# A two-layer hybrid encoder on one core: in the first half of the feed-forward, raw low halves of the weights go to GpSimd, unions of product banks precede the next weights' sums, and ScalarE copies the second bank whole

## The chip, the core and the metric

The kernel runs on one core of one Trainium2 chip, in one launch. The time is the device time of one execution in microseconds (us). The core's engines work beside each other, each through its own list of instructions in order: TensorE (PE; PEld is its loading of weights), VectorE (DVE), ScalarE (ACT), GpSimd (POOL) and SyncE (SP), which issues the DMA transfers. They wait for each other through semaphores. SBUF is the on-chip memory; PSUM is the memory into which TensorE writes its products, in banks of 128x512 fp32 numbers. GpSimd's instructions here have all their operands in SBUF; VectorE and ScalarE read and write both memories.

## What is computed

The input is x of shape (1, 512, 1024) in fp32, and the parameters of two layers. The feed-forward part, in which the change lies, closes each layer:

```python
        hf = rms_norm(x, ffn_norm_g[l])
        u = depthwise_conv(hf @ ffn_w_up[l], ffn_conv_w[l], ffn_conv_b[l])
        u_gate, u_val = u[..., :D_FF], u[..., D_FF:]
        x = x + (jax.nn.silu(u_gate) * u_val) @ ffn_w_down[l]
```

D_FF is 2816, so the up projection is 1024 to 5632 and the down projection 2816 to 1024. Ahead of it stand, in each layer, an RMS norm, a combined input projection, three branches (multi-head latent attention, grouped-query attention, centred mean pooling), their gated merge and an output projection.

## The kernel before

**Layout.** The stream x is held transposed in SBUF as XM, eight tiles of 128 channels by 512 tokens. The normed input of the up projection is held as HH (high half) and HL (low half).

**Products in three parts.** Each fp32 operand is split in two fp32r numbers, high and low, and a product is taken as high by high, high by low and low by high. The weights come from HBM as raw pieces (128x512, two to a transfer of 512 KB; three transfers' room, filled by SP). ScalarE copies a raw piece into `wh` (L272), and VectorE or GpSimd makes `wl` as raw minus `wh` (L280). L272 and L280 are helpers through which nearly every copy and every two-operand operation goes, so groups are told apart by their tiles.

**Seven products for eight.** Most of the feed-forward's pieces are used in a Strassen-like form (`w_seven`): a piece holds a 2x2 block of 128x128 tiles and is used with seven products, not eight. Its first three blocks are used as they are: ScalarE copies them (`wh<-raw`, 128x384), and `rest` makes their low halves (`wl<-raw,wh`, 128x384), on the engine that `pick(W_BIAS)` chooses. The other four weights are sums of blocks: `first` has ScalarE copy one block into a PSUM bank (`ps_mi` or `ps_S`, in turn), `both`, `third` and `fourth` build the sums there on VectorE (one 128x256 and two 128x128 operations), `hi` copies the bank to `wh` (128x512, ScalarE) and `lo` makes `wl<-ps_mi,wh` or `wl<-ps_S,wh` (128x512, VectorE). In the names of the order, `wh180_0` and `wl180_0` are the raw part of piece 180, `wh180_1` and `wl180_1` its sums.

**Halves.** The 22 blocks of D_FF are done in two halves, 10 and 12 (HALVES). In each half the up projection runs first, then the down projection over four pairs of output tiles (m = 0, 2, 4, 6): five pieces for each m in the first half, six in the second. `products` (matmuls at L1911) runs 21 matmuls of 128x256 for each piece into four PSUM banks b0 to b3, which are drawn from a ring of six (two each of acc, ST and AV). With the first piece of an m the banks are taken in the order b0, b1, b2, b3, b2 at its 13th matmul and b3 at its 19th. The last piece of m = 0 runs the products in the order 2, 1, 3, 6, 5, 4, 7 (`late`), with the activations that come last used last.

**Unite.** When an m is done, `unite` adds its four banks into two XM tiles and gives the banks back to the ring: XM += b0 (b0 free); ScalarE copies the first half of b1 into u; u2 (the second half of u) = first half + second half of b1 on VectorE (b1 free); XM += b2 in two operations (b2 free); b3 += u2; XM += u on GpSimd; XM += b3 (b3 free). For the last m of the program an `early` form has all of it on VectorE.

**Back loads.** In the first half the normed input is fetched again during the down projection (`again(m)`): four tiles `back` for each m, split into HH and HL or tf by ScalarE and GpSimd, spaced by GAP.

**Activations.** `up_evac` takes the up projection's output through convolution and gate and splits it into `ah` tiles; `turns` makes two of the splits (of t34 and t12), for the last block of D_FF on VectorE, else on GpSimd.

**What sets the order.** A planner runs at build time. It keeps a clock for each engine with estimated costs, takes steps of `chain`s from a heap as their inputs are expected to be ready, and emits instructions in that order; data dependencies then become semaphore waits. On the chip each engine follows the emitted order.

Of the kernel before, what the change touches and what calls it, by code (L numbers as in the profile page):

```python
# [63 lines left out]
GAP = 2.0  # L64
# [93 lines left out]
class Clock:  # L158
# [5 lines left out]
    def __init__(self):  # L164
        self.now, self.n, self.heap, self.busy = 0.0, 0, [], False
        self.fin, self.free, self.ready = 0.0, {}, {}
        self.source = self.last = None
        self.gives_way = {}
        self.locked = (0.0, 0.0)
# [50 lines left out]
    def chain(self, *steps, after=0.2):  # L220

        def go(n, source=None, since=None):
# [4 lines left out]
            if late and max(late) > self.now:  # L227
                self.at(max(late) - self.now, lambda: go(n))
                return
# [84 lines left out]
def trunk(ctx: ExitStack, tc: tile.TileContext, x, w, prm, gb, cst, pad, out):  # L314
# [99 lines left out]
    def w_seven():  # L414
# [20 lines left out]
        def rest():  # L435
            e = pick(W_BIAS)
            e.tensor_tensor(los[0][:, :384], r[:, :384], f(his[0][:, :384]), ALU.subtract)
            done("wa", j)
            if j + 1 == len(pieces) or pieces[j + 1][0] > sl:
                at(max(0.0, ck.free[e.kind] - ck.now) + D_FREE, lambda: w_upto(sl + 1 + RAW))  # L440
# [17 lines left out]

        chain(([("sums", j * L // len(pieces))] + ([("w", j - 2)] if seven[j - 2] else []), first), rest, after=0.0)
# [202 lines left out]
    def layer(l, sq, xsrc):  # L662
# [206 lines left out]
        def set_keys():  # L869
            for _, kb in KAB:  # L870
                G.memset(f(kb[64:P, :T]), 0.0)
                G.memset(f(kb[64:65 if "gqa" in PLAN else 96, :T]), 1.0)

        at(0.5, set_keys)
# [918 lines left out]
        def up_evac(c, part, acc, tag, scaled):  # L1793
# [77 lines left out]
            def turns():  # L1871
# [3 lines left out]
                      *split(new[4][:, :T], new[5][:, :T], t34[:, :T], eng=eng), end(2), after=0.0)  # L1875
# [12 lines left out]
        def products(right_, banks_, first, late=False):  # L1888
            j = st["use"]
            his, los = (lambda z: (z[:2], z[2:]))(wnext())  # L1890
# [81 lines left out]
        def unite(m, banks_, then, early=False):  # L1972
# [11 lines left out]
            chain(lambda: A.activation(p1, b1[:, :256], AF.Copy), after=0.0)  # L1984
            if early:
                chain(add(x0, x0, b0), add(u2, p1, b1[:, hi_]), add(x0[:, hi_], x0[:, hi_], b2[:, hi_]), add(x0, x0, u[:, :T]),
# [3 lines left out]
            chain(add(x0, x0, b0), lambda: free(t0), add(u2, p1, b1[:, hi_]), lambda: free(t1),  # L1990
                  add(x0[:, hi_], x0[:, hi_], b2[:, hi_]), add(x1, x1, b2), lambda: free(t2),
                  add(b3[:, :256], u2, b3[:, :256]),
# [29 lines left out]
        for c0, c1 in HALVES:  # L2022
            room[:] = spare
            for n_, (c, part) in enumerate(_ups(c0, c1)):
# [15 lines left out]
            for m in range(0, KC, 2):  # L2040
# [4 lines left out]
                for k in range(c0, c1 - 2 * PLAIN * end_, 2):  # L2045
                    products(right_of(k // 2), banks_, k == c0, m == 0 and k == c1 - 2)
# [211 lines left out]
```

## Time and profile before

| | |
|---|---|
| median of 3 runs (lowest to highest) | 1538.01 us (1537.58 to 1538.58) |
| the profiled execution's own time | 1538.08 us |
| its span, first to last instruction | 1536.3 us |
| DVE, ACT, POOL busy | 1206.2, 974.5, 1120.1 us (79%, 63%, 73%) |
| mean granted TensorE clock | 0.999 |
| HBM traffic over the span | 118 GB/s |
| chain that ended last, by engine | PE 75%, DVE 12%, ACT 6%, POOL 3%, issue 3%, DMA 1% |

The profiled execution lies 0.07 us from the median, and 1.78 us of its time lie outside the span. In the rows of the timeline, the first number is the start in us from the span's start, the second the duration (of a row with x2 or more, from the start of the first to the end of the last), then engine, line, operation, tiles written <- tiles read, shape, and how many. What stands in square brackets is idle time of the engine before the row, and what ended it. A matmul's duration overlaps with the next one's: the time that it costs is the distance from start to start.

### The profile page before, as it was taken

What the parts mean: (1) busy time and instruction counts of PE and PEld (TensorE: products, weight loads), DVE (VectorE), ACT (ScalarE), POOL (GpSimd) and SP (SyncE); (2) the same over time, 40 slices, a digit from 0 to 9 for tenths busy, and PEclk for the clock granted to TensorE, in tenths of its full rate; (3) what the DMA queues carried; (4) which work ended last, traced back from release to release, by engine and by line L of the source; (5) the groups of instructions that cost most, each with busy time, mean ns of one, the idle gap of its engine ahead of it and who ended that gap; (6) DMA issues with size and microseconds to landing.
All of it is one profiled execution on the core that took longest, in us unless ns stands there. A gap on an engine that the chain in (4) does not pass through costs nothing.

```text
span 1536.3 us, 25158 instructions
## 1 busy us (share of the span) xinstructions
PE 1519.1 (99%) x8390; PEld 1325.6 (86%) x8390; DVE 1206.2 (79%) x2386; ACT 974.5 (63%) x1961; POOL 1120.1 (73%) x1077
## 2 busy tenths in 40 slices
PE   9999999999999999999999999999999999999999
PEld 8888788788889899999998877888888899989998
DVE  6778889986578896778857788899865788867786
ACT  6557776664567665666654587766636677656763
POOL 4865986854689787675779659868547897967753
PEclk9999999999999999999999999999999999999999
DMA  6432234424344453333444322344243444533332
GB/s 219 117 111 78 76 92 139 130 91 132 105 140 147 148 176 106 94 103 109 133 129 136 102 70 76 112 134 130 79 151 96 141 148 138 182 107 100 95 121 84
DMA packets 91954, 183.56 MB, mean 119 GB/s; under 512 B 21936, under 2 KB 43696, under 8 KB 91824
## 3 DMA queue, kind: packets, MB, share of 16 engines
q1 hardware_dynamic: 91680, 181.94, 38.0%
q8 instruction: 66, 1.08, 0.3%
q14 instruction: 64, 0.52, 0.1%
q10 hardware_dynamic: 144, 0.01, 0.0%
HBM read 159.89 MB, written 22.02 MB: 118 GB/s over the span
## 4 chain that ended last, share of the span: by engine, by line
PE 75%; DVE 12%; ACT 6%; POOL 3%; issue 3%; DMA 1%; SPq 0%; ACTq 0%; DVEq 0%; POOLq 0%
PE ps_acc L491 24%; PE ps_AV L491 16%; PE ps_ST L1911 8%; PE ps_ST L491 8%; PE ps_acc L1911 7%; PE ps_AV L1911 6%; PE ps_S L491 2%; PE ps_mi L491 2%; ACT wh L272 2%; DVE nmt L290 1%; DVE wl L280 1%; DVE vt L284 1%; DVE XM L280 1%; DVE pl L280 1%; POOL qa L280 1%
## 5 line engine op out<-in xcount | busy, mean ns | idle before, releaser
L280 POOL TENSOR_TENSOR wl<-raw,wh 128x512 fp32r<-128x512 f32 (+3 forms) x487 | 579.7, 1200 | 306.3 <-ACT wh L272 267.0
L272 ACT ACTIVATE wh<-raw 128x512 fp32r<-128x512 f32 (+2 forms) x521 | 290.9, 577 | 21.1 <-PE ps_ST L491 11.3
L491 PE MATMUL ps_acc<-HH,wh 128*128 128x512 f32 x504 | 196.9, 391 | 0.1
L491 PE MATMUL ps_acc<-HL,wh 128*128 128x512 f32 x504 | 196.5, 390 | 0.0
L491 PE MATMUL ps_acc<-HH,wl 128*128 128x512 f32 x504 | 196.3, 389 | 0.0
L491 PEld LDWEIGHTS ps_acc<-HH,wl 128*128 128x128 f32 x504 | 94.6, 188 | 19.9
L491 PEld LDWEIGHTS ps_acc<-HH,wh 128*128 128x128 f32 x504 | 94.7, 188 | 19.7 <-DVE gt L280 0.6
L491 PEld LDWEIGHTS ps_acc<-HL,wh 128*128 128x128 f32 x504 | 94.7, 188 | 18.9
L491 PE MATMUL ps_AV<-HH,wh 128*128 128x512 f32 x248 | 96.7, 390 | 0.0
L491 PE MATMUL ps_AV<-HL,wh 128*128 128x512 f32 x248 | 96.6, 390 | 0.0
L491 PE MATMUL ps_AV<-HH,wl 128*128 128x512 f32 x248 | 96.5, 389 | 0.0
L272 ACT ACTIVATE wh<-ps_S 128x512 fp32r<-128x512 f32 x79 | 47.3, 598 | 49.2 <-DVE ps_S L280 37.8
L272 ACT ACTIVATE wh<-ps_mi 128x512 fp32r<-128x512 f32 x79 | 47.3, 598 | 46.5 <-DVE ps_mi L280 38.1
L280 DVE TENSOR_TENSOR wl<-ps_mi,wh 128x512 fp32r<-128x512 f32 x79 | 54.0, 684 | 12.2 <-ACT wh L272 10.6
L280 POOL TENSOR_TENSOR a<-a,cv 128x511 f32<-128x511 f32 x36 | 46.8, 1314 | 21.9 <-DVE a L284 21.9
L280 DVE TENSOR_TENSOR wl<-ps_S,wh 128x512 fp32r<-128x512 f32 x79 | 54.0, 684 | 10.6 <-ACT wh L272 9.7
L272 ACT ACTIVATE gt<-gt 128x512 f32<-128x512 f32 x48 | 30.2, 628 | 43.3 <-DVE gt L280 43.1
L1911 PE MATMUL ps_acc<-ah,wh 128*128 128x256 f32 x276 | 56.5, 283 | 0.0
L1911 PE MATMUL ps_ST<-ah,wh 128*128 128x256 f32 x294 | 55.5, 284 | 0.3 <-ACT wh L272 0.2
L290 DVE TENSOR_REDUCE nm<-ps_S 128x1 f32<-128x512 f32 x64 | 43.6, 682 | 15.1 <-PE ps_S L491 14.6
L272 ACT ACTIVATE ps_ST<-ps_ST 128x512 f32<-128x512 f32 x74 | 42.3, 583 | 20.1 <-PE ps_ST L491 12.4
L491 PEld LDWEIGHTS ps_AV<-HH,wl 128*128 128x128 f32 x248 | 46.6, 188 | 9.8
(560 smaller groups left out, 5201.2 us busy)
## 6 DMA issues: line engine op xcount, KB each, us to landing
raw<-w SPq DMA_DIRECT2D x228, 512.0 KB, 3.6
raw<-w SPq DMA_DIRECT2D x13, 384.0 KB, 3.1
XM<-x SPq DMA_DIRECT2D x16, 256.0 KB, 3.6
back<-hsp SPq DMA_DIRECT2D x16, 256.0 KB, 3.9
back<-tsp SPq DMA_DIRECT2D x16, 256.0 KB, 4.3
dtq<-tr SPq DMA_DIRECT2D x16, 192.0 KB, 1.9
dtk<-tr SPq DMA_DIRECT2D x16, 192.0 KB, 2.0
tf<-dtq SPq DMA_DIRECT2D x48, 64.0 KB, 2.1
```

Of the source, the lines that this page charges most:

```text
L272: return self.eng.activation(out, in_, func, **k)
L280: return self.eng.tensor_tensor(out, *a)
L284: return self.eng.scalar_tensor_tensor(out, *a)
L290: return self.eng.tensor_reduce(out, in_, *a, **k)
L491: PE.matmul(o, lhsT=lhsT, rhs=rhs, start=start, stop=stop)
L1911: PE.matmul(banks_[b][1][:, 256 * at_:256 * at_ + 256], lhsT=(his, his, los)[q][i][:, ws], rhs=right[n][q == 1], start=first and b not in ...
```

## The change

Six edits, in the planner's rules and in the code of the feed-forward, and one at the start of the attention:

- `rest` (the low halves of a piece's raw part, 128x384) goes to GpSimd throughout the first half, up and down projection, in place of the engine that `pick` chose; the same flag acts in `w_split` for the plain pieces of the up projection.
- `hi` and `lo` of later pieces are put off by the planner while an m's last piece is in its last 0.65 us and until 0.15 us after its end (HOLD), so that the operations of `unite` come ahead of them in the engines' orders.
- `unite` (not its `early` form): ScalarE copies the whole bank b1 into u (128x512, before 128x256) and b1 is free after this copy; u2 = u's two halves added, on GpSimd from SBUF (before on VectorE with the second half read from PSUM).
- GAP, the planner's spacing of the four splits of the back loads, is 3 in place of 2.
- The split of t34 for the last block of D_FF makes its low half on GpSimd in place of VectorE.
- The constants of the attention's key tiles (`kb`, four memsets in each layer) are set by VectorE, planned at 4.0, in place of GpSimd at 0.5.

```diff
--- before.py
+++ after.py
@@ -61,7 +61,9 @@
 D_OUT, D_IN, D_LAT = 3.2, 4.0, 6.0
 D_FREE, D_SUM = 0.8, (2.0, 0.8)
 REST = 0.4
-GAP = 2.0
+GAP = 3.0
+ONLY = True
+HOLD = (0.65, 0.15)
 PREP = (2, 5, 8, 11)
 W_BIAS = 2.54
 C_BIAS = 0.0
@@ -165,7 +167,7 @@
         self.now, self.n, self.heap, self.busy = 0.0, 0, [], False
         self.fin, self.free, self.ready = 0.0, {}, {}
         self.source = self.last = None
-        self.gives_way = {}
+        self.gives_way, self.waits, self.pause = {}, set(), (0.0, 0.0)
         self.locked = (0.0, 0.0)
 
     def low(self, fn, most=4.0, engine="DVE"):
@@ -226,6 +228,9 @@
             late = [self.ready.get(k, self.now + 0.5) for k in keys]
             if late and max(late) > self.now:
                 self.at(max(late) - self.now, lambda: go(n))
+                return
+            if fn in self.waits and self.pause[0] <= self.now < self.pause[1] - 0.001:
+                self.at(self.pause[1] - self.now, lambda: go(n, source, since))
                 return
             eng, most = self.gives_way.get(fn, (None, 0.0))
             since = self.now if since is None else since
@@ -433,7 +438,7 @@
             A.activation(his[0][:, :384], r[:, :384], AF.Copy)
 
         def rest():
-            e = pick(W_BIAS)
+            e = G if pool_only[0] else pick(W_BIAS)
             e.tensor_tensor(los[0][:, :384], r[:, :384], f(his[0][:, :384]), ALU.subtract)
             done("wa", j)
             if j + 1 == len(pieces) or pieces[j + 1][0] > sl:
@@ -456,6 +461,7 @@
             V.tensor_tensor(los[1], s[0], f(his[1]), ALU.subtract)
             done("w", j)
 
+        ck.waits.update((hi, lo))
         chain(([("sums", j * L // len(pieces))] + ([("w", j - 2)] if seven[j - 2] else []), first), rest, after=0.0)
         chain(([("a21", j)], both), third, fourth, hi, lambda: done("wh", j), lo, after=0.01)
         halves[j] = his + los
@@ -868,10 +874,10 @@
 
         def set_keys():
             for _, kb in KAB:
-                G.memset(f(kb[64:P, :T]), 0.0)
-                G.memset(f(kb[64:65 if "gqa" in PLAN else 96, :T]), 1.0)
-
-        at(0.5, set_keys)
+                V.memset(f(kb[64:P, :T]), 0.0)
+                V.memset(f(kb[64:65 if "gqa" in PLAN else 96, :T]), 1.0)
+
+        at(4.0, set_keys)
 
         at(14.0, set_ones)
         tok_major(gqb, T)
@@ -1872,7 +1878,7 @@
                 eng = V if c + 1 == FC else G
                 w0 = whole.pop(p)
                 chain(diff(t3, 1, w0[:, 256:T], ALU.add), diff(t4, 0, t2, ALU.subtract), qfree,
-                      *split(new[4][:, :T], new[5][:, :T], t34[:, :T], eng=eng), end(2), after=0.0)
+                      *split(new[4][:, :T], new[5][:, :T], t34[:, :T], eng=G), end(2), after=0.0)
                 chain(*split(new[2][:, :T], new[3][:, :T], t12[:, :T], eng=eng), end(1), after=0.0)
 
             w0 = whole[p]
@@ -1885,8 +1891,10 @@
             bh, bl, ah, al, ch, cl, dh, dl = act[kp]
             return (bh, bl), (ah, al), (ch, cl), (dh, dl), ("acth", l, kp), *[("act", l, kp, k) for k in range(3)]
 
-        def products(right_, banks_, first, late=False):
+        def products(right_, banks_, first, late=False, end=False):
             j = st["use"]
+            if end:
+                ck.pause = (ck.now + 2.52 - HOLD[0], ck.now + 2.52 + HOLD[1])
             his, los = (lambda z: (z[:2], z[2:]))(wnext())
             (bh, bl), (ah, al), (ch, cl), (dh, dl), kb, ka, kc_, kd = right_
             lo_, hi_ = slice(0, 256), slice(256, T)
@@ -1981,15 +1989,16 @@
             def add(o, y_, z, e=V):
                 return lambda: e.tensor_tensor(o, y_, z, ALU.add)
 
-            chain(lambda: A.activation(p1, b1[:, :256], AF.Copy), after=0.0)
             if early:
+                chain(lambda: A.activation(p1, b1[:, :256], AF.Copy), after=0.0)
                 chain(add(x0, x0, b0), add(u2, p1, b1[:, hi_]), add(x0[:, hi_], x0[:, hi_], b2[:, hi_]), add(x0, x0, u[:, :T]),
                       add(x1, x1, b2), add(b3[:, :256], u2, b3[:, :256]),
                       lambda: V.tensor_tensor(pair(x1), pair(x1), b3[:, None, :256].to_broadcast([P, 2, 256]), ALU.add), after=0.0)
                 return
-            chain(add(x0, x0, b0), lambda: free(t0), add(u2, p1, b1[:, hi_]), lambda: free(t1),
+            chain(lambda: A.activation(u[:, :T], b1, AF.Copy), lambda: free(t1), add(u2, p1, u2, G), lambda k=c0: done("u2", l, m, k), after=0.0)
+            chain(add(x0, x0, b0), lambda: free(t0),
                   add(x0[:, hi_], x0[:, hi_], b2[:, hi_]), add(x1, x1, b2), lambda: free(t2),
-                  add(b3[:, :256], u2, b3[:, :256]),
+                  ([("u2", l, m, c0)], add(b3[:, :256], u2, b3[:, :256])),
                   add(x0, x0, u[:, :T], G), lambda: then and then(m),
                   lambda: V.tensor_tensor(pair(x1), pair(x1), b3[:, None, :256].to_broadcast([P, 2, 256]), ALU.add), lambda: free(t3),
                   lambda: then and then(m + 1), after=0.0)
@@ -2021,6 +2030,7 @@
 
         for c0, c1 in HALVES:
             room[:] = spare
+            pool_only[0] = ONLY and not c0
             for n_, (c, part) in enumerate(_ups(c0, c1)):
                 if not c0 and n_ in PREP:
                     scaled_pair(2 * PREP.index(n_))
@@ -2043,7 +2053,7 @@
                     again(m)
                 end_ = last and c1 == FC and m == KC - 2
                 for k in range(c0, c1 - 2 * PLAIN * end_, 2):
-                    products(right_of(k // 2), banks_, k == c0, m == 0 and k == c1 - 2)
+                    products(right_of(k // 2), banks_, k == c0, m == 0 and k == c1 - 2, k == c1 - 2)
                 unite(m, banks_, finish if c1 == FC else None, end_)
                 if end_:
                     free("mi")
```

The sequence of TensorE's instructions stays as it is but for the names of banks. VectorE has 16 instructions fewer, GpSimd 16 more, ScalarE and SP as many as before in a slightly other order.

The first place is the change from m = 2 to m = 4 in layer 0's first half, on VectorE. Pieces 178 to 180 are the last of m = 2, 181 is the first of m = 4; ps_AV_880 and the banks with the next numbers hold the sums of m = 2. Before:

```order
L280 TENSOR_TENSOR ps_S_751_4840<-raw93_6206,ps_S_751_4840 128x128 x2
L280 TENSOR_TENSOR wl180_1_6373<-ps_mi_750_4839,wh180_1_6371 128x512
L280 TENSOR_TENSOR wl181_1_6410<-ps_S_751_4840,wh181_1_6408 128x512
L280 TENSOR_TENSOR ps_mi_750_4839<-ps_mi_750_4839,raw94_6321 128x256
L280 TENSOR_TENSOR wl182_0_6447<-raw94_6321,wh182_0_6445 128x384
L280 TENSOR_TENSOR ps_mi_750_4839<-raw94_6321,ps_mi_750_4839 128x128 x2
L280 TENSOR_TENSOR XM_80<-XM_80,ps_AV_880_6295 128x512
L280 TENSOR_TENSOR wl182_1_6448<-ps_mi_750_4839,wh182_1_6446 128x512
L280 TENSOR_TENSOR u2_884_6480<-u2_884_6480,ps_AV_881_6300 128x256
```

And with the change:

```order
L285 TENSOR_TENSOR ps_S_751_4840<-raw93_6206,ps_S_751_4840 128x128 x2
L285 TENSOR_TENSOR wl181_1_6411<-ps_S_751_4840,wh181_1_6409 128x512
L285 TENSOR_TENSOR ps_mi_750_4839<-ps_mi_750_4839,raw94_6320 128x256
L285 TENSOR_TENSOR ps_mi_750_4839<-raw94_6320,ps_mi_750_4839 128x128 x2
L285 TENSOR_TENSOR XM_80<-XM_80,ps_AV_880_6292 128x512
L285 TENSOR_TENSOR XM_80<-XM_80,ps_ST_882_6314 128x256
L285 TENSOR_TENSOR ps_S_751_4840<-ps_S_751_4840,raw94_6320 128x256
L285 TENSOR_TENSOR XM_80<-XM_80,ps_ST_882_6314 128x512
L285 TENSOR_TENSOR ps_S_751_4840<-raw94_6320,ps_S_751_4840 128x128
L285 TENSOR_TENSOR wl182_1_6445<-ps_mi_750_4839,wh182_1_6443 128x512
```

The raw low half wl182_0 and the add into u2 are gone from VectorE, and the union's adds of b0 and b2 stand ahead of wl182_1.

The second place is GpSimd at the same time. Before:

```order
L280 TENSOR_TENSOR HL_82<-back_877_6281,HH_81 128x512
L280 TENSOR_TENSOR wl181_0_6409<-raw93_6206,wh181_0_6407 128x384
L280 TENSOR_TENSOR tf_873_6276<-back_878_6283,tf_872_6275 128x512
L280 TENSOR_TENSOR tf_875_6278<-back_879_6285,tf_874_6277 128x512
L280 TENSOR_TENSOR wl183_0_6495<-raw94_6321,wh183_0_6493 128x384
L280 TENSOR_TENSOR wl184_0_6536<-raw95_6389,wh184_0_6534 128x384
L280 TENSOR_TENSOR XM_80<-XM_80,u2_884_6480 128x512
```

With the change:

```order
L285 TENSOR_TENSOR HL_82<-back_877_6278,HH_81 128x512
L285 TENSOR_TENSOR wl181_0_6410<-raw93_6206,wh181_0_6408 128x384
L285 TENSOR_TENSOR tf_873_6273<-back_878_6280,tf_872_6272 128x512
L285 TENSOR_TENSOR wl182_0_6444<-raw94_6320,wh182_0_6442 128x384
L285 TENSOR_TENSOR u2_884_6477<-u2_884_6477 128x256
L285 TENSOR_TENSOR wl183_0_6492<-raw94_6320,wh183_0_6490 128x384
L285 TENSOR_TENSOR tf_875_6275<-back_879_6282,tf_874_6274 128x512
L285 TENSOR_TENSOR XM_80<-XM_80,u2_884_6477 128x512
```

Two operations have come in, wl182_0 and the add into u2, and the second tf is two rows later.

The third place is the end of m = 0 in layer 0's second half, on VectorE. Piece 242 is the last of m = 0; ah_1030 is the low half of t34. Before:

```order
L280 TENSOR_TENSOR ah_1028_8335<-t12_1023_8330,ah_1027_8334 128x512
L280 TENSOR_TENSOR ah_1026_8333<-ps_acc_1021_8282,ah_1025_8332 128x512
L280 TENSOR_TENSOR ah_1030_8337<-t34_1024_8331,ah_1029_8336 128x512
L280 TENSOR_TENSOR wl241_1_8419<-ps_S_751_4840,wh241_1_8417 128x512
L280 TENSOR_TENSOR ps_mi_750_4839<-ps_mi_750_4839,raw124_8252 128x256
L280 TENSOR_TENSOR ps_mi_750_4839<-raw124_8252,ps_mi_750_4839 128x128
L280 TENSOR_TENSOR ps_S_751_4840<-ps_S_751_4840,raw124_8252 128x256
L280 TENSOR_TENSOR ps_mi_750_4839<-raw124_8252,ps_mi_750_4839 128x128
L280 TENSOR_TENSOR ps_S_751_4840<-raw124_8252,ps_S_751_4840 128x128 x2
L280 TENSOR_TENSOR wl242_1_8460<-ps_mi_750_4839,wh242_1_8458 128x512
```

With the change:

```order
L285 TENSOR_TENSOR ah_1028_8335<-t12_1023_8330,ah_1027_8334 128x512
L285 TENSOR_TENSOR ah_1026_8333<-ps_acc_1021_8282,ah_1025_8332 128x512
L285 TENSOR_TENSOR wl241_1_8419<-ps_S_751_4840,wh241_1_8417 128x512
L285 TENSOR_TENSOR ps_mi_750_4839<-ps_mi_750_4839,raw124_8252 128x256
L285 TENSOR_TENSOR ps_mi_750_4839<-raw124_8252,ps_mi_750_4839 128x128 x2
L285 TENSOR_TENSOR ps_S_751_4840<-ps_S_751_4840,raw124_8252 128x256
L285 TENSOR_TENSOR ps_S_751_4840<-raw124_8252,ps_S_751_4840 128x128 x2
L285 TENSOR_TENSOR wl242_1_8460<-ps_mi_750_4839,wh242_1_8458 128x512
```

The low half of t34 has left VectorE (on GpSimd it stands ahead of wl242_0), and the three operations that build piece 242's sums in ps_mi stand together.

## The prediction, made before the changed kernel ran

> **What bounds the kernel now.** I read the page's busy times first, then the table of waits of TensorE, then the timeline around the waits that name the lines of the change.
>
> ```profile
> PE 1519.1 (99%) x8390; PEld 1325.6 (86%) x8390; DVE 1206.2 (79%) x2386; ACT 974.5 (63%) x1961; POOL 1120.1 (73%) x1077
> ...
> PE ps_AV L1911 <- DVE XM L280: 2.5, 2, 1.3
> ...
> PE ps_ST L1911 <- DVE XM L280: 1.0, 2, 0.6
> ...
> PE ps_ST L1911 <- DVE wl L280: 0.6, 2, 0.4
> PE ps_AV L1911 <- DVE u L280: 0.4, 2, 0.2
> PE ps_ST L1911 <- ACT wh L272: 0.2, 1, 0.2
> ```
>
> TensorE is busy 99% of the span. The change doesn't touch its instructions, so all that can be won is idle time of TensorE in the down projections (L1911), a few microseconds in these five rows, and all that can be lost is new idle time. The largest row is two waits for an XM add, up to 1.3 us each. In layer 0 the timeline has it here:
>
> ```profile
> 558.34 0.40 PE L1911 MATMUL ps_ST<-sMK,wh 128*128 128x256 f32 x2
> 558.58 0.28 PE L1911 MATMUL ps_ST<-sMK,wl 128*128 128x256 f32 x1
> ...
> 559.66 0.28 PE L1911 MATMUL ps_acc<-sMK,wl 128*128 128x256 f32 x1
> 561.20 0.51 PE L1911 MATMUL ps_AV<-sMQ,wh 128*128 128x256 f32 x2 [1.26 <-DVE XM L280]
> ...
> 561.90 0.28 PE L1911 MATMUL ps_AV<-sMK,wl 128*128 128x256 f32 x1
> 562.37 0.50 PE L1911 MATMUL ps_AV<-sMQ,wh 128*128 128x256 f32 x2 [0.20 <-DVE u L280]
> ```
>
> Two matmuls cost 0.24 us from start to start (558.34 to 558.58), so one costs 0.12. After 559.66 the next start is 1.54 later, 1.42 too late; and the first two matmuls behind a pause last 0.51 where others last 0.40, another 0.1. So the first stall costs 1.52, the second (0.47 less 0.12, and 0.1) 0.45; together **1.98 us**. Bank b2 of m = 4 waits for the add that empties b0 of m = 2, and b3 waits for the add into u2 that empties b1. What held VectorE:
>
> ```profile
> 556.09 3.93 DVE L280 TENSOR_TENSOR wl<-raw,wh 128x384 fp32r<-128x384 f32 x1
> 559.94 0.61 DVE L280 TENSOR_TENSOR ps_mi<-raw,ps_mi 128x128 f32<-128x128 f32 x2
> 560.47 0.68 DVE L280 TENSOR_TENSOR XM<-XM,ps_AV 128x512 f32<-128x512 f32 x1
> ...
> 561.91 0.41 DVE L280 TENSOR_TENSOR u<-u,ps_AV 128x256 f32<-128x256 f32 x1
> ...
> 556.08 1.01 POOL L280 TENSOR_TENSOR wl<-raw,wh 128x384 fp32r<-128x384 f32 x1
> 557.05 2.55 POOL L280 TENSOR_TENSOR tf<-back,tf 128x512 fp32r<-128x512 f32 x2
> ```
>
> One raw low half took 3.93 us on VectorE. It ended 0.4 after GpSimd's unbroken row of work (557.05 + 2.55 = 559.60) had ended. Both inputs and the output of that operation lie in SBUF. Operations of VectorE with an input in PSUM were not drawn out beside an equally busy GpSimd:
>
> ```profile
> 546.00:558.60 12.60, 12.60 (x108) 12.60 (x107) 11.57 (x24) 8.13 (x20) 12.60 (x12) 1.00 0.44 135
> ...
> L280 DVE TENSOR_TENSOR wl<-ps_S,wh x10: 670/687/693, 527.8 to 578.0; 128x512 fp32r<-128x512 f32 x10
> ...
> L280 DVE TENSOR_TENSOR wl<-raw,wh x3: 1147/1886/3932, 524.3 to 583.4; 128x384 fp32r<-128x384 f32 x2, 128x512 fp32r<-128x512 f32 x1
> ```
>
> The columns of the first row are the stretch and its length, the busy time of PE, PEld, DVE, ACT and POOL, the granted clock, the DMA's share and GB/s. GpSimd was busy for all 12.60 us, and the ten `wl<-ps_S` last 670 to 693 ns, while the three `wl<-raw` last 1147 to 3932. So I take it that only operations with both inputs in SBUF wait for GpSimd, and the sum has no term for the others. The Trainium skill (SBUF — State Buffer, Who interferes with whom) says the same: a VectorE instruction with two SBUF inputs contends with GpSimd's reads, one with at most one doesn't, and who starts second is blocked. By that rule, the trace agrees; were all of VectorE held up by what GpSimd gets more (eight adds of 0.70 and four low halves of 0.97, both priced below, 9.5 us), the sum would end 3 us slower.
>
> **The change part by part: first halves.** In the down projections of the first half no operation of VectorE with two SBUF inputs is left (each row of the changed order there has a ps tile). So the 3.93 us go from VectorE, and it gets to the b0 add with the end of m = 2's last matmul at 558.34: the add takes 0.68, so b0 is free at about 559.1 to 559.4, and b2 of m = 4 is wanted 12 matmuls after 558.34, at 559.78. For b3, wanted at 558.34 + 18 x 0.12 = 560.50, ScalarE's whole copy of b1 (about 0.60 in place of 0.38) now stands ahead of wh182_1, behind nothing that waits. Both stalls go: −1.98. Layer 1 has the same pair:
>
> ```profile
> 1318.66 3.92 DVE L280 TENSOR_TENSOR wl<-raw,wh 128x384 fp32r<-128x384 f32 x1
> ...
> 1323.75 0.50 PE L1911 MATMUL ps_AV<-sMQ,wh 128*128 128x256 f32 x2 [1.23 <-DVE XM L280]
> ```
>
> The pause is 0.03 shorter (the second one is in the 0.4 us, two waits, of the table), so −1.95. Sum of the first halves: **−3.93**.
>
> What pays for it is GpSimd, whose rows in the first half's down projection of layer 0 are:
>
> ```profile
> L280 POOL TENSOR_TENSOR wl<-raw,wh 128x384 fp32r<-128x384 f32 x17 | 17.3, 1021 | 7.5 <-ACT wh L272 7.4
> L280 POOL TENSOR_TENSOR HL<-back,HH 128x512 fp32r<-128x512 f32 x8 | 10.4, 1301 | 0.0
> ...
> 709.69 0.74 POOL L280 TENSOR_TENSOR t<-a 128x256 f32<-128x256 f32 x1
> ```
>
> From start to start a raw low half costs 0.97 (556.08 to 557.05), a 128x512 operation some 1.27 (two in 2.55), the 128x256 add into u2 some 0.70 (0.74 less the overlap of 0.04 that the low halves show). An m has five pieces of 21 x 0.12 = 2.52, 12.6 us, and GpSimd has in it 5 x 0.97 + 4 x 1.27 (back loads) + 1.27 (XM += u) + 0.70 = **11.9 us, 94%**. It fits, with little room. I went through its changed order from 546 on, each operation after the one before and after its input: wl180_0 is done at 555.5 and wanted at 556.06 (three matmuls into its piece), wl181_0 at 557.7 against 558.6, wl182_0 at 560.0 against 561.1, wl183_0 at 561.6 against 563.6. The least room is 0.57. GAP = 3 puts the back splits up to 3 us later in the plan, which the up projection of the second half reads much later. In the queue of SP the `back` transfers and raw pieces of a layer change places by one at most, and pieces are in a buffer well before use. Cost: 0, hidden under TensorE; without that cover each late low half would cost its lateness plus 0.1.
>
> **Second halves.** They keep `pick`, but have the new `unite`, the holding, and the moved split of t34.
>
> ```profile
> 719.34 0.40 PE L1911 MATMUL ps_ST<-ah,wh 128*128 128x256 f32 x2
> ...
> 719.94 0.28 PE L1911 MATMUL ps_ST<-ah,wl 128*128 128x256 f32 x1
> 720.44 0.50 PE L1911 MATMUL ps_ST<-ah,wh 128*128 128x256 f32 x2 [0.22 <-ACT wh L272]
> 721.16 0.39 PE L1911 MATMUL ps_ST<-ah,wl 128*128 128x256 f32 x1 [0.22 <-DVE wl L280]
> ...
> 724.79 0.51 PE L1911 MATMUL ps_ST<-sMQ,wh 128*128 128x256 f32 x2 [0.37 <-DVE XM L280]
> ...
> 717.19 0.68 DVE L280 TENSOR_TENSOR ah<-t,ah 128x512 fp32r<-128x512 f32 x1
> 717.79 0.68 DVE L280 TENSOR_TENSOR wl<-ps_S,wh 128x512 fp32r<-128x512 f32 x1
> ...
> 720.42 0.69 DVE L280 TENSOR_TENSOR wl<-ps_mi,wh 128x512 fp32r<-128x512 f32 x1 [0.21 <-ACT wh L272]
> ```
>
> Reckoned as above, the three stalls cost 0.48, 0.49 and 0.64 (idle 0.37, the 0.16 by which a pause in brackets falls short of the lost start, as 1.26 against 1.42, and 0.1): 1.61. Without the `ah<-t` VectorE is 0.60 earlier (717.19 to 717.79). Then wh242_1 comes in time, but wl242_1, done at 720.42 + 0.69 − 0.60 = 720.5 for the ninth matmul of the piece at 719.34 + 0.96 = 720.30, is still late: 0.2 + 0.1 = 0.3. The third stall came from the add of b0, behind a `wl`; now the copy of b1 by ScalarE frees that place at about 723.6, wanted at 723.6. I take it as gone, and keep 0.4 for the range. Layer 0: −1.3.
>
> ```profile
> 1480.71 0.74 PE L1911 MATMUL ps_ST<-ah,wh 128*128 128x256 f32 x4
> ...
> 1483.99 0.39 PE L1911 MATMUL ps_ST<-ah,wl 128*128 128x256 f32 x1 [0.37 <-DVE wl L280]
> 1487.86 0.50 PE L1911 MATMUL ps_ST<-sMQ,wh 128*128 128x256 f32 x2 [0.62 <-DVE XM L280]
> ```
>
> In layer 1 the stalls at 1480.71 (0.36), 1481.87 (0.21), 1483.99 (0.64) and 1487.86 (0.88) make 2.09. The first waits for ScalarE, whose order is unchanged there: stays. The second and fourth go, the third shrinks to about 0.44: −1.3. The add into u2 moves from VectorE (0.41 from PSUM) to GpSimd (0.74), which has idle time before its low halves here; b3's add waits for it, and b3 is wanted 0.72 after b2.
>
> **The memsets.** Ahead of the attention VectorE is idle where the constants go now:
>
> ```profile
> 48.06 2.15 POOL L310 MEMSET kb<- 64x512 f32 x4
> 52.38 1.13 DVE L280 TENSOR_TENSOR win<-win,C 128x8 f32<-128x8 f32 x2 [3.84 <-POOL win L280]
> ```
>
> 2.15 us of GpSimd against an idle 3.84 of VectorE, at a place where TensorE waits for neither: 0, at worst +0.5 a layer if an operation behind them is late.
>
> **Sum**: 3.93 + 1.3 + 1.3 = 6.5 us. The profiled execution took 1538.08 and the median is 1538.01, so either base gives **1531.5**. All 7.63 of these stalls gone would give 1530.4.
>
> **The rivals.**
>
> *The second halves give nothing*: banks freed by ScalarE's copy, which stands behind a `wh` that waits for VectorE's sums, are as late as by the adds before (the two times of 723.6 lie on each other), and the held `hi` and `lo` come late in their turn. Then 1538.0 − 3.9 = **1534.1**. For it speaks the lack of room, against it the 0.60 us that VectorE sheds ahead of it.
>
> *The load moves without effect.* The Trainium skill (Perfetto Trace Analysis, Optimizing Scalar/DVE Operations) warns that moving work between VectorE and GpSimd may not help, as they share a port of SBUF. As a mechanism of this kernel: another operation of VectorE takes the long wait, the first halves' 3.93 stays, and only the 2.6 of the second halves come: **1535.4**. Against it: no operation with two SBUF inputs stands in the order at 556 to 562.
>
> *GpSimd becomes the bound of the first half.* In its order the add into u2 waits for ScalarE's copy of b1, which waits for the last matmul into b1, and behind it stand the low halves of the next pieces (wl183_0, then the XM add and wl184_0). While it waits GpSimd does nothing. An m leaves it 12.6 − 11.9 = 0.7; from a wait of more than that for each m, with the 0.57 of room used up, the low halves come late in every later piece. At 1.5 us late for each of the eight unions (about what the b0 add is late now) TensorE loses 12 less the 6.5 won: **1543.5**, slower. For it speaks the 94%; against it that ScalarE was idle for 4.6 us at this place before and that the copy now stands ahead of wh182_1.
>
> ```profile
> 560.67 0.60 ACT L272 ACTIVATE wh<-ps_mi 128x512 fp32r<-128x512 f32 x1 [4.62 <-DVE ps_mi L280]
> ```
>
> **How the numbers follow.** A run of this kernel can be told from no change at about 0.2%, 3.1 us, so faster means under 1534.9. Forecast 0.58 (1530 to 1533.3); second halves give nothing, or half of it, 0.22 (1533.3 to 1535, most of it faster); load without effect 0.08 (1535.4, same); GpSimd the bound 0.12, of which a mild form, a late piece here and there, gives no change (0.03) and the full one is slower (0.09). So faster 0.78, same 0.13, slower 0.09. The range from 1529.6 to 1537.0 leaves out the slower case and a little of the mild one.
>
> **What would show it right or wrong.** In the changed profile the waits `ps_AV L1911 <- DVE XM` and `<- DVE u` are gone from the first halves; VectorE has no `wl<-raw` over 1 us between 521 and 572; GpSimd is over 90% busy there; the waits of the second halves shrink to about 1 us in all. It is wrong if TensorE shows waits `<- POOL wl` at L1911 (the GpSimd rival), or if the XM waits stay with another long row of VectorE ahead of them, or if the time is above 1535.

## The result and the profile after

The changed kernel takes **1531.42 us** (median of 6 runs, 1530.79 to 1532.37) against 1537.67 of the kernel before beside it (6 runs, 1537.11 to 1538.58): ratio 0.9959, interval 0.9947 to 0.9972, so 4 to 8 us faster, 6.25 by the medians. 1531.5 was forecast. The profiled execution took 1531.25 us with a span of 1529.5, 6.8 less than before.

TensorE's work is the same, and the first line of the page shows where the load went: 13 us from VectorE, 13 us to GpSimd.

```profile
PE 1517.1 (99%) x8390; PEld 1326.3 (87%) x8390; DVE 1193.2 (78%) x2370; ACT 977.3 (64%) x1961; POOL 1133.5 (74%) x1093
```

In the table of TensorE's waits (engine, tile and line; who releases it; us in total, times, longest) the down projections' line, now L1919, has two rows left of five:

```profile
PE ps_ST L1919 <- ACT wh L277: 0.2, 1, 0.2
PE ps_ST L1919 <- DVE wl L285: 0.2, 1, 0.2
```

To set the places side by side I added up, from the trace, how much later than usual each matmul starts behind the one before it (distance from start to start, less the lower quartile of the distances between matmuls of the same two shapes). That counts a pause and the slow start behind it:

| us lost by TensorE | before | after | change |
|---|---|---|---|
| layer 0, around the first half's down projection (520 to 582) | 1.99 | 0.03 | −1.96 |
| layer 1, the same place (1280 to 1345) | 2.00 | 0.06 | −1.94 |
| layer 0, second half (713 to 765) | 1.63 | 0.57 | −1.06 |
| layer 1, second half (1470 to the end) | 2.15 | 0.97 | −1.18 |
| all the rest | 26.3 | 25.7 | −0.6 |

The four places make 6.14 of the span's 6.8. The rest moves by as much between executions of one kernel: a second profile of the changed kernel has 26.7 there.

At the change from m = 2 to m = 4 in layer 0 the timeline of the changed kernel reads:

```profile
556.67 0.62 DVE L285 TENSOR_TENSOR ps_mi<-raw,ps_mi 128x128 f32<-128x128 f32 x2
557.98 0.69 DVE L285 TENSOR_TENSOR XM<-XM,ps_AV 128x512 f32<-128x512 f32 x1 [0.68 <-PE ps_AV L1919]
558.77 0.42 DVE L285 TENSOR_TENSOR XM<-XM,ps_ST 128x256 f32<-128x256 f32 x1
...
557.51 1.30 POOL L285 TENSOR_TENSOR tf<-back,tf 128x512 fp32r<-128x512 f32 x1
558.76 1.02 POOL L285 TENSOR_TENSOR wl<-raw,wh 128x384 fp32r<-128x384 f32 x1
559.74 0.74 POOL L285 TENSOR_TENSOR u<-u 128x256 f32<-128x256 f32 x1
560.43 1.01 POOL L285 TENSOR_TENSOR wl<-raw,wh 128x384 fp32r<-128x384 f32 x1
...
558.10 0.60 ACT L277 ACTIVATE u<-ps_AV 128x512 f32<-128x512 f32 x1 [1.48 <-PE ps_AV L1919]
...
558.14 0.40 PE L1919 MATMUL ps_ST<-sMK,wh 128*128 128x256 f32 x2
...
559.58 0.40 PE L1919 MATMUL ps_AV<-sMQ,wh 128*128 128x256 f32 x2
...
560.30 0.40 PE L1919 MATMUL ps_AV<-sMQ,wh 128*128 128x256 f32 x2
```

VectorE now waits 0.68 us for TensorE's last product into b0, where before TensorE waited for VectorE. The add of b0 is over at 558.67 and ScalarE's copy of b1 at 558.70. Matmuls 13 and 19 of the new m start at 559.58 and 560.30, 1.44 and 2.16 behind 558.14, which is 12 and 18 steps of 0.12: no pause. GpSimd is full, as the same stretches in windows show (stretch, length, busy time of PE, PEld, DVE, ACT, POOL):

```profile
546.00:558.60 12.60, 12.60 (x107) 12.60 (x106) 10.07 (x25) 8.18 (x20) 12.60 (x12) 1.00 0.42 129
558.60:571.20 12.60, 12.60 (x107) 12.60 (x106) 10.43 (x26) 8.61 (x22) 12.60 (x13) 1.00 0.69 238
```

12.60 of 12.60 us, twice in a row, and TensorE isn't held up: no row of the waits names GpSimd at L1919. In the first of them VectorE's busy time fell from 11.57 to 10.07, for a good part the long operation's blocked time. VectorE's operations with an operand in PSUM aren't drawn out beside this full GpSimd: the ten `wl` that it makes from PSUM between 546 and 571 last 682 to 693 ns.

What is left in layer 0's second half:

```profile
718.29 0.39 PE L1919 MATMUL ps_ST<-ah,wl 128*128 128x256 f32 x1
...
721.26 0.28 PE L1919 MATMUL ps_acc<-sMK,wl 128*128 128x256 f32 x1
721.61 0.51 PE L1919 MATMUL ps_acc<-sMQ,wh 128*128 128x256 f32 x2
...
720.48 0.60 ACT L277 ACTIVATE wh<-ps_mi 128x512 fp32r<-128x512 f32 x1 [1.48 <-PE ps_AV L1919]
720.97 0.59 ACT L277 ACTIVATE u<-ps_acc 128x512 f32<-128x512 f32 x1
```

A bank is still late at 721.61, by 0.23 and 0.1: it is the one that the whole copy of b1 frees (720.97 + 0.59 = 721.56), and this copy stands behind a `wh` that ScalarE could start only after 1.48 us of idling.

### The profile page after: what moved, and what is told of

It is laid out like the page before. It is cut to its first block, busy times and chain, and to the rows that moved or that the text cites. A ratio compares the mean times of both kernels' runs of the same rounds, so it can differ in the third digit from the quotient of the medians.

```text
span 1529.5 us, 25179 instructions
## 1 busy us (share of the span) xinstructions
PE 1517.1 (99%) x8390; PEld 1326.3 (87%) x8390; DVE 1193.2 (78%) x2370; ACT 977.3 (64%) x1961; POOL 1133.5 (74%) x1093
## 4 chain that ended last, share of the span: by engine, by line
PE 86%; DVE 6%; ACT 3%; POOL 3%; issue 1%; POOLq 0%; DVEq 0%; ACTq 0%
PE ps_acc L497 28%; PE ps_AV L497 17%; PE ps_ST L1919 10%; PE ps_ST L497 9%; PE ps_acc L1919 9%; PE ps_AV L1919 7%; PE ps_S L497 2%; PE ps_mi L497 2%; DVE nmt L295 1%; POOL qa L285 1%; DVE pl L285 1%; PE ps_ST L1460 1%; DVE vt L289 1%; DVE XM L285 1%; ACT ps_ST L277 1%
## 5 line engine op out<-in xcount | busy, mean ns | idle before, releaser
L285 POOL TENSOR_TENSOR wl<-raw,wh 128x512 fp32r<-128x512 f32 (+2 forms) x494 | 586.6, 1197 | 280.0 <-ACT wh L277 254.5
L285 DVE TENSOR_TENSOR wl<-ps_mi,wh 128x512 fp32r<-128x512 f32 x79 | 54.1, 685 | 11.9 <-ACT wh L277 11.0
L1919 PE MATMUL ps_ST<-ah,wh 128*128 128x256 f32 x298 | 59.9, 284 | 0.2 <-ACT wh L277 0.2
L1919 PE MATMUL ps_acc<-ah,wh 128*128 128x256 f32 x276 | 55.0, 283 | 0.0
```

The source lines that it names most:

```text
L285: return self.eng.tensor_tensor(out, *a)
L1919: PE.matmul(banks_[b][1][:, 256 * at_:256 * at_ + 256], lhsT=(his, his, los)[q][i][:, ws], rhs=right[n][q == 1], start=first and b not in ...
```

## The experiments

The runs were made four at a time, on three occasions; those of one occasion share the runs of the kernel before, so each is set against that median (1538.16 for the first four, 1538.55 for the next four, 1538.64 for the last four). The changed kernel itself stood at −6.25 and −6.50. The four columns to the right are TensorE's lost time at the four places, as in the table above; they come from one profile each and tell small edits apart where the medians don't. The two profiles of the changed kernel differ by 0.07 and 0.16 us in the last two columns, so less than that says nothing.

| run | median | to before | L0 first | L1 first | L0 second | L1 second |
|---|---|---|---|---|---|---|
| before | | 0 | 1.99 | 2.00 | 1.63 | 2.15 |
| the change (first profile) | 1531.42 | −6.25 | 0.03 | 0.06 | 0.57 | 0.97 |
| e1 one operation moved | 1533.54 | −4.62 | 0.03 | 0.06 | 1.70 | 2.29 |
| e2 it put back | 1531.98 | −6.18 | 0.23 | 0.27 | 0.69 | 0.91 |
| e3 flag off | 1530.83 | −7.33 | 0.03 | 0.06 | 0.32 | 0.98 |
| e4 t34 on VectorE | 1532.47 | −5.69 | 0.03 | 0.06 | 0.99 | 1.30 |
| e5 old union | 1531.40 | −7.15 | 0.03 | 0.06 | 0.25 | 0.92 |
| e6 no holding | 1534.28 | −4.27 | 0.03 | 0.06 | 2.27 | 1.54 |
| e7 old memsets | 1531.61 | −6.94 | 0.03 | 0.06 | 0.59 | 0.99 |
| e8 t12 on GpSimd too | 1532.30 | −6.25 | 0.03 | 0.06 | 0.43 | 1.34 |
| e9 one operation, holding | 1533.51 | −5.13 | 0.03 | 0.06 | 1.04 | 1.83 |
| e10 and t34 | 1532.68 | −5.96 | 0.03 | 0.06 | 0.35 | 1.24 |
| e11 and t12 | 1532.95 | −5.69 | 0.03 | 0.06 | 1.11 | 1.38 |
| e12 the change again | 1532.14 | −6.50 | 0.03 | 0.06 | 0.64 | 1.13 |

**e1: one operation a layer moved, from the kernel before.**

```diff
-            e = pick(W_BIAS)
+            e = G if j in (182, 443) else pick(W_BIAS)
```

> The kernel before, with one operation of each layer moved: the raw low half of piece 182 (443 in layer 1) is made by GpSimd, not VectorE; unions, holding and all else as before. Theory (the first halves' stalls hang on VectorE's one long operation, which waits for GpSimd's reads): both stalls at the change from m = 2 to m = 4 go in both layers, 3.94 us, the second halves' 3.7 us stay; 1533.8 against 1537.7. Rival (the union's order and the copy by ScalarE are needed too): the add of b0 stays late, at most 1 us is won, 1536.7 or more.

Measured: ratio 0.9974 (0.9965 to 0.9983), 4.6 us off by the medians, and both first halves are free of pauses. VectorE and GpSimd at the place:

```profile
555.83 0.63 DVE L280 TENSOR_TENSOR ps_mi<-raw,ps_mi 128x128 f32<-128x128 f32 x2
557.20 0.69 DVE L280 TENSOR_TENSOR wl<-ps_mi,wh 128x512 fp32r<-128x512 f32 x1 [0.75 <-ACT wh L272]
557.90 0.69 DVE L280 TENSOR_TENSOR XM<-XM,ps_AV 128x512 f32<-128x512 f32 x1
...
556.74 2.60 POOL L280 TENSOR_TENSOR tf<-back,tf 128x512 fp32r<-128x512 f32 x2
559.25 3.04 POOL L280 TENSOR_TENSOR wl<-raw,wh 128x384 fp32r<-128x384 f32 x3
```

The add of b0 stands behind wl182_1, with the old union and no holding, and is in time at 557.90. The theory holds: the first halves' 3.9 us hung on this one operation of each layer, and no other edit is needed for them.

**e2: the same operation put back, in the changed kernel.**

```diff
-            e = G if pool_only[0] else pick(W_BIAS)
+            e = V if j in (182, 443) else G if pool_only[0] else pick(W_BIAS)
```

> The changed kernel with wl182_0 and wl443_0 put back on VectorE. Theory (it waits for a pause of GpSimd): with the second tf split and the add into u2 further back in GpSimd's order, GpSimd pauses before the add into u2, at about 558.9, and the operation ends then, after 2.5 to 3 us instead of 3.9; the stall at bank b2 comes back in part, 0.2 to 0.6 us a layer, 1531.9 to 1532.6. Rival (the operation is slow there by itself): 3.9 us again and 1.5 us of stall a layer, 1534.5. Second rival (slow only by chance of the other order): 0.6 us, no stall, 1531.4.

```profile
556.96 2.58 DVE L285 TENSOR_TENSOR wl<-raw,wh 128x384 fp32r<-128x384 f32 x1
559.46 0.61 DVE L285 TENSOR_TENSOR ps_mi<-raw,ps_mi 128x128 f32<-128x128 f32 x2
...
556.81 1.05 POOL L285 TENSOR_TENSOR wl<-raw,wh 128x384 fp32r<-128x384 f32 x1
557.78 1.33 POOL L285 TENSOR_TENSOR tf<-back,tf 128x512 fp32r<-128x512 f32 x1
559.07 1.06 POOL L285 TENSOR_TENSOR u<-u 128x256 f32<-128x256 f32 x1
```

It lasts 2.58 us, not 3.93: it ends 0.43 after GpSimd's `tf` (557.78 + 1.33 = 559.11), and the next operation of GpSimd, an add of 0.74 in the changed kernel, takes 1.06. Each engine waited for the other. The pause that comes back is 0.2 us a layer. The duration follows what GpSimd does beside it; the operation is neither slow by itself nor quick by another order. One part of the theory isn't borne out: it had GpSimd pause before the add into u2, but the add starts as `tf` ends, and the operation of VectorE gets through there without a pause.

**e3: the flag for GpSimd alone off.**

```diff
-ONLY = True
+ONLY = False
```

> The changed kernel with the flag for GpSimd alone off (ONLY = False). By the order of instructions only wl171_0 and wl432_0, the first pieces of the first halves, go back to VectorE; wl182_0 is given to GpSimd by the planner's own choice now. Theory: those two were never late, so nothing: 1531.4, with one operation over 1 us on VectorE in each layer and no new wait. Rival (any raw low half on VectorE beside GpSimd costs TensorE): 0.5 us a layer or more, 1532.4.

The places are as with the change (0.32 against 0.57 and 0.64 is the pause for the bank, which is there or not by a tenth of a microsecond), with one operation of 1.14 us on VectorE in each layer. The flag does nothing for the time that these runs show: the planner's own choice already takes piece 182 from VectorE once the rest of the order has changed.

**e4: t34's low half on VectorE again.**

```diff
-                      *split(new[4][:, :T], new[5][:, :T], t34[:, :T], eng=G), end(2), after=0.0)
+                      *split(new[4][:, :T], new[5][:, :T], t34[:, :T], eng=eng), end(2), after=0.0)
```

> The changed kernel with the split of t34 for the last block on VectorE again. Theory (this 0.6 us on VectorE is what the second halves' first waits hang on): the wait for wh at the last piece of m = 0 comes back, 0.3 to 0.5 us in layer 0 and 0.1 to 0.3 in layer 1, and the wait for wl grows by 0.3: 1532.2 to 1532.6; the waits at bank b2 of m = 2 stay as they are with the change. Rival (the second halves' gain is all the union's): 1531.4, the waits unchanged.

```profile
PE ps_ST L1919 <- DVE wl L285: 0.6, 2, 0.4
PE ps_ST L1919 <- ACT wh L277: 0.2, 1, 0.2
```

The waits for `wl` are 0.6 in place of 0.2; the places lose 0.42 and 0.33 us more than with the change. The step is worth 0.75 us in all, just under what was expected. No wait for a bank came back with it, so it wasn't t34's move that ended those.

**e5: the old union, in the changed kernel.**

```diff
-            chain(lambda: A.activation(u[:, :T], b1, AF.Copy), lambda: free(t1), add(u2, p1, u2, G), lambda k=c0: done("u2", l, m, k), after=0.0)
-            chain(add(x0, x0, b0), lambda: free(t0),
+            chain(lambda: A.activation(p1, b1[:, :256], AF.Copy), after=0.0)
...
+            chain(add(x0, x0, b0), lambda: free(t0), add(u2, p1, b1[:, hi_]), lambda: free(t1),
```

> The changed kernel with the old union: ScalarE copies half of b1, VectorE makes u2 from PSUM. Theory (in the second halves bank b1 must be free early, and the copy on ScalarE does it): at the first piece of m = 2 the wait for a bank grows from 0.33 to about 0.8 us in layer 0 and comes back with 0.6 to 0.9 in layer 1; the first halves stay free of waits: 1532.5 to 1533. Rival (VectorE has room enough once t34 is off it, the copy adds nothing): 1531.4.

The theory fell. No wait for a bank is there in either layer (the waits are the two rows of the changed kernel), and layer 0 loses 0.25, less than the 0.57 and 0.64 of the change. ScalarE's whole copy of b1 wins nothing here, and costs the 0.33 us at 721.61 that the first section shows.

**e6: no holding.**

```diff
-        ck.waits.update((hi, lo))
```

> The changed kernel without the holding of hi and lo. By the order the add of b0 then stands behind wl182_1 in the first half (as in the run with one operation moved, which had no wait there) and behind wl244_1 in the second. Theory: no wait in the first halves; in the second halves the bank of b0 comes 0.6 us later, 0.3 to 0.7 us of TensorE's time a layer: 1532.0 to 1532.8. Rival (the holding only reorders work that has room): 1531.4.

```profile
PE ps_ST L1918 <- ACT u L277: 0.5, 1, 0.5
PE ps_AV L1918 <- ACT u L277: 0.5, 1, 0.5
...
736.28 0.28 PE L1918 MATMUL ps_AV<-sMK,wl 128*128 128x256 f32 x1
737.04 0.50 PE L1918 MATMUL ps_ST<-sMQ,wh 128*128 128x256 f32 x2 [0.49 <-ACT u L277]
...
735.91 0.60 ACT L277 ACTIVATE wh<-ps_mi 128x512 fp32r<-128x512 f32 x1 [1.22 <-DVE ps_mi L285]
736.40 0.59 ACT L277 ACTIVATE u<-ps_ST 128x512 f32<-128x512 f32 x1
```

Slower than the change by 2 us (−4.27 against −6.25 and −6.50). The first halves have no wait, as expected. But what is late isn't the add of b0, nor at m = 2: it is ScalarE's copy of b1, at the changes to m = 4 and to m = 6 of layer 0's second half, where it stands behind `wh`, which waits for VectorE's sums. At m = 2, where the kernel before lost 0.63 and 0.88 us, only 0.16 us a layer are lost without the holding: there the copy (720.43 + 0.59 = 721.02 in layer 0) frees its bank before the 13th matmul, at 721.13. So the holding is what makes room for the new union at the later changes; without it the whole copy opens waits of its own.

**e7: the memsets on GpSimd again.**

```diff
-                V.memset(f(kb[64:P, :T]), 0.0)
...
-        at(4.0, set_keys)
+                G.memset(f(kb[64:P, :T]), 0.0)
...
+        at(0.5, set_keys)
```

> The changed kernel with the four memsets of each layer on GpSimd again (by the order wl20 goes back to VectorE with it). Theory: they are covered, 1531.4 within 0.4. Rival (the time that the change won outside the down projections comes from them): 0.5 us slower or more, 1531.9.

1531.61, the four places as with the change. They are covered, either way.

**e8: t12's low half on GpSimd too, in the changed kernel.**

```diff
-                chain(*split(new[2][:, :T], new[3][:, :T], t12[:, :T], eng=eng), end(1), after=0.0)
+                chain(*split(new[2][:, :T], new[3][:, :T], t12[:, :T], eng=G), end(1), after=0.0)
```

> The changed kernel with the low half of t12 for the last block on GpSimd too, as t34 is. Theory (the second halves' last waits, 0.6 us in layer 0 and 0.9 in layer 1, hang on VectorE's work ahead of the last piece of m = 0): VectorE is another 0.6 us earlier, and by the order ScalarE's copy of b1 comes ahead of wh244_1; most of the 1.5 us goes: 1530.2 to 1530.6. Rival (GpSimd, with two operations of 1.3 us in a row there, makes wl242_0 or the halves of t12 late): new waits for POOL, 1531.4 or more.

```profile
PE ps_acc L1919 <- ACT u L277: 0.6, 1, 0.6
PE ps_ST L1919 <- ACT wh L277: 0.2, 1, 0.2
```

No waits for `wl` are left at these lines, and none for GpSimd, against the rival; but banks are late at m = 2: 0.87 us are lost in layer 1, where ScalarE's copy stands behind a `wh` again, and 0.31 in layer 0, by the add of b0. Nothing is won.

**e9: from the kernel before, the one operation and the holding.** GAP, union, t34, flag and memsets are as before; of the holding this is the core:

```diff
-            e = pick(W_BIAS)
+            e = G if j in (182, 443) else pick(W_BIAS)
...
+        ck.waits.update((hi, lo))
...
+            if end:
+                ck.pause = (ck.now + 2.52 - HOLD[0], ck.now + 2.52 + HOLD[1])
```

> The kernel before with two edits alone: wl182_0 and wl443_0 on GpSimd, and the holding of hi and lo; the old union, t34 on VectorE, no other edit. Theory (the holding, not ScalarE's copy, ends the waits for a bank in the second halves): the first halves free of waits, the bank waits at the first piece of m = 2 (0.63 and 0.88 us) gone, the waits at the last piece of m = 0 as before (0.97 and 1.2 us): 1532.2 to 1532.6. Rival (the bank waits went with t34's move): 1533.7, as with the one operation alone.

```profile
PE ps_ST L1918 <- ACT wh L276: 0.7, 2, 0.5
PE ps_ST L1918 <- DVE wl L284: 0.6, 2, 0.4
```

No row with XM or u: the two waits for a bank, of 0.63 and 0.88 us before, are gone with the old union and t34 on VectorE, by the holding alone: e1, which differs from this run only by the holding, still has them (0.63 and 0.89). The waits at the last piece of m = 0 stay, as the theory has it, and the one in layer 1 is longer (0.71 against 0.36). −5.13, where −5.1 to −5.5 was expected.

**e10: and t34 on GpSimd.**

```diff
-                      *split(new[4][:, :T], new[5][:, :T], t34[:, :T], eng=eng), end(2), after=0.0)
+                      *split(new[4][:, :T], new[5][:, :T], t34[:, :T], eng=G), end(2), after=0.0)
```

> The same with a third edit, t34's low half on GpSimd. Theory: these three are the whole change, 1531.4 within 0.4, the waits of the second halves 0.2 to 0.3 in layer 0 and 0.9 in layer 1 as in the run with the old union. Rival (the union, GAP, the flag or the memsets carry a part): 1532 or more.

−5.96, beside −6.50 of the change on the same occasion. Layer 0's second half is at 0.35 (0.64 with the change), layer 1's at 1.24 (1.13). At the four places the three edits do as much as the six. By the medians they are 0.5 us behind, with ranges that overlap (1532.42 to 1533.66, 1532.05 to 1532.58), and the four places account for no part of it; whether that half microsecond is real stays open.

**e11: and t12 on GpSimd.** The edit of e8 on top.

> The three edits and t12's low half on GpSimd as well. Theory: without ScalarE's whole copy of b1 the waits for a bank that the run with t12 and the new union had (0.31 and 0.87 us) don't come, and the waits for wl are gone: left is the wait for wh in layer 1, 0.45 us; 1530.3 to 1530.8, under the changed kernel by 0.6 to 1.1. Rival (any shift of VectorE's work opens another wait): 1531.4 or more.

```profile
717.89 0.69 DVE L284 TENSOR_TENSOR wl<-ps_mi,wh 128x512 fp32r<-128x512 f32 x1 [0.75 <-PE ps_AV L1918]
718.50 0.42 DVE L284 TENSOR_TENSOR ps_S<-ps_S,raw 128x256 f32<-128x256 f32 x1
...
720.34 0.69 DVE L284 TENSOR_TENSOR wl<-ps_S,wh 128x512 fp32r<-128x512 f32 x1 [0.75 <-PE ps_AV L1918]
...
721.94 0.68 DVE L284 TENSOR_TENSOR XM<-XM,ps_ST 128x512 f32<-128x512 f32 x1
...
722.67 0.50 PE L1918 MATMUL ps_ST<-sMQ,wh 128*128 128x256 f32 x2 [0.78 <-DVE XM L284]
```

The last three operations of VectorE, as they stand in the changed kernel:

```profile
716.56 0.43 DVE L285 TENSOR_TENSOR ps_S<-ps_S,raw 128x256 f32<-128x256 f32 x1
...
718.39 0.69 DVE L285 TENSOR_TENSOR wl<-ps_S,wh 128x512 fp32r<-128x512 f32 x1 [0.15 <-ACT wh L277]
...
719.99 0.68 DVE L285 TENSOR_TENSOR XM<-XM,ps_ST 128x512 f32<-128x512 f32 x1
```

The theory fell: the waits for `wl` are gone, but waits for a bank have come, of 1.04 us in layer 0 and of 0.26 and 0.46 in layer 1. In layer 0 the planner, with VectorE freer, put wl242_1 (717.89) ahead of the next sums in ps_S. VectorE stands idle for 0.75 us ahead of it, waiting for TensorE, so these sums start 1.94 later, wl243_1 and, behind them all, the add of b0 as much later, where TensorE wants the bank only 0.35 later than in the changed kernel.

**e12: the changed kernel again.**

> The changed kernel itself beside them: 1531.4 within 0.5, waits as in its first profile (0.59 us in layer 0's second half, 0.9 in layer 1's).

1532.14, 0.7 above its first runs, as the kernel before was higher too on that occasion (1538.64 against 1537.67); waits as in its first profile. None of the variants can be told to be faster than it.

## Why the prediction was right, point by point

**The first halves, −3.93: right, and shown.** The places lost 3.99 us before and 0.09 now. One operation of each layer explains all of it (e1), and its length follows GpSimd's work (e2). That the two engines hold each other up is measured; through what they do so no run separates. What the prediction left unsaid is that the flag isn't what moves the operation: with it off the planner moves it as well (e3).

**GpSimd's 11.9 us in 12.6: right.** Over the four m it is busy for 46.75 of 50.40 us in layer 0 and 46.71 in layer 1, 93%. The load isn't even: it has gaps during m = 0 and none for more than 25 us after it, with nothing late. The four low halves that were to end at 555.5, 557.7, 560.0 and 561.6 end at 555.31, 557.54, 559.78 and 561.44, and TensorE too is 0.20 earlier (558.14 for 558.34), so the room is about as reckoned. The rival in which GpSimd stands waiting for the copy didn't come: it reached the add into u2 at 559.74, a microsecond after the copy's end, and at all eight unions of the first halves it came 0.3 us or more after it. Its fullness is itself what kept it from waiting there. In the second halves it does wait for the copy, 0.6 to 1.9 us at each union, and has the time for it.

**t34, right in place and size.** The wait that should stay in layer 0 at 0.3 is 0.26 (718.29), those of layer 1 foreseen at 0.36 and 0.44 are 0.46 and 0.45. For the 0.44 the prediction gives no working. Putting t34 back costs 0.75 us (e4).

**The waits for a bank in the second halves: the term that was mis-sized.** The prediction had "now the copy of b1 by ScalarE frees that place at about 723.6, wanted at 723.6. I take it as gone". In the changed kernel the copy does free that bank, but it is over at 721.56 where the bank is wanted at 721.38, and 0.33 us are lost in layer 0, within the 0.4 kept for the range. So the second halves gave 1.06 + 1.18 = 2.2 us where 2.6 were summed. Nor is the copy needed for what was won. The holding alone, with the old union, ends both waits (e9 against e1), and with the old union in the changed kernel the 0.33 is gone as well (e5). With the copy and without the holding little is lost at m = 2, but 0.86 and 0.73 us are lost at the two later changes of layer 0, where the kernel before lost nothing (e6). The prediction names the holding among the edits and gives it no price of its own; that step it left out.

**The rest.** Memsets at 0: right (e7). The flag and GAP need not be there for the first halves to be free of waits (e9, e10 have neither); GAP alone wasn't tried.

**The signs.** The XM and u waits of the first halves are gone, VectorE has no raw low half left between 521 and 572, and no row names GpSimd at L1919. Two signs are off. GpSimd is busy for 42.59 of the 51 us from 521 to 572, 84%, not over 90%, since that stretch begins in the up projection, 12 us ahead of the down projection. And the second halves still lose 1.5 us, not about 1.

**The sum.** 6.5 against 6.25 by the medians and 6.1 at the four places. That 1531.5 and 1531.42 lie so close is in part luck: the kernel before was 0.34 lower beside the changed one than the 1538.01 that the sum starts from, which makes up for the 0.25 by which the gain fell short. (The three stalls of layer 0 come to 1.59 by the prediction's own formula, not 1.61, which changes nothing.) The rivals "second halves give nothing", "load without effect" and "GpSimd the bound" didn't come about.

## What to carry to other kernels

A short wait of the bounding engine can hang on one operation that was given to the wrong engine at one place: look for the same form with a duration several times its usual one, and see what the other engines did meanwhile, before touching the order around it. An engine that is 100% busy over a stretch isn't a bound as long as each of its results is in time; reckon the room of each, not the share. And when an edit adds a copy to free a buffer sooner, look at what the copying engine has to do just ahead of it: here the order of the work was enough without the copy, and the copy was not enough without the order.

## What the hardware showed beside it

VectorE's raw low half (both inputs in SBUF) can miss several ends of GpSimd's operations in a row. Its usual length with GpSimd idle is at the start of the kernel before, in the summary of its tile; the rows behind it are of two places further on, where GpSimd is at work beside it, and of GpSimd's first operation after the long one:

```profile
L280 DVE TENSOR_TENSOR wl<-raw,wh x8: 550/558/559, 4.4 to 18.1; 128x384 fp32r<-128x384 f32 x8
...
524.32 1.15 DVE L280 TENSOR_TENSOR wl<-raw,wh 128x384 fp32r<-128x384 f32 x1
...
655.86 1.30 DVE L280 TENSOR_TENSOR wl<-raw,wh 128x384 fp32r<-128x384 f32 x1
...
523.75 1.30 POOL L280 TENSOR_TENSOR wl<-raw,wh 128x512 fp32r<-128x512 f32 x1 [2.66 <-ACT wh L272]
525.00 2.88 POOL L280 TENSOR_TENSOR a<-a,cv 128x511 f32<-128x511 f32 x2
...
562.23 1.01 POOL L280 TENSOR_TENSOR wl<-raw,wh 128x384 fp32r<-128x384 f32 x1 [2.62 <-ACT wh L272]
...
656.68 1.63 POOL L280 TENSOR_TENSOR ah<-t,ah 128x512 fp32r<-128x512 f32 x1
```

Alone it takes 0.56 us. At 524.32 and 655.86 it got its turn when GpSimd's running operation ended (523.75 + 1.30 = 525.05), and the next one of GpSimd was longer for it (1.63 in place of 1.3). At 556.09 it passed two such ends, at about 557.1 and 558.3, and ended only 0.4 us after GpSimd's last; in e2 it passed one and took the second. The Trainium skill (SBUF — State Buffer, SBUF: two separate sides) says that whichever of the two engines starts first holds the ports that they share for its whole instruction, and that the other is blocked. The trace agrees that each can block the other: 1.15 to 3.93 us in place of 0.56 on VectorE, 1.63 and 1.06 in place of 1.30 and 0.74 on GpSimd. It shows more than one instruction's wait, though, since VectorE's operation was passed over at two ends. In the kernel before, GpSimd had nothing to do for 2.62 us behind the end at which the operation got through (the row at 562.23); in e2 and at the two places above it had a next operation at once, and VectorE got its turn all the same. Why it wins the turn at some ends and not at others isn't settled by these runs.
